# A two-layer hybrid encoder trunk: keys, values and first queries projected before the gate input

## The chip, the cores and the metric

One core of one Trainium2 chip. Times are device microseconds (us) of a whole execution. The kernel before takes 1126.06 us, the median of three runs (1125.95 to 1127.46).

## The reference, cut to what matters

Each of the two layers normalises its input, projects it to 1792 columns and splits them into queries, keys and values for an attention group and two gate inputs for a gating group:

```python
h = rms_norm(x, attn_norm_g[i])
proj = h @ w_in[i]
q, k, v, u, vv = jnp.split(proj, split_at, axis=-1)
q = axial_rope(rms_norm(q.reshape(b, s, N_HEADS, HEAD_DIM), q_norm_g[i]), tables)
k = axial_rope(rms_norm(k.reshape(b, s, N_KV_HEADS, HEAD_DIM), k_norm_g[i]), tables)
attn_o = gqa_attention(q, k, v)
sg_o = spatial_gating(jax.nn.gelu(u), jax.nn.gelu(vv), sg_norm_g[i], sg_w[i], sg_b[i])
merged = concatenate([rms_norm(attn_o, attn_out_g[i]), rms_norm(sg_o, sg_out_g[i])])
x = x + merged @ w_o[i]
# then a second norm, an up-projection, a depthwise convolution, SiLU gate, a down-projection
```

There are 512 positions, width 1024, 8 query heads and 2 key/value heads of 64, and 8 gating heads of 64. `spatial_gating` norms vv per head and mixes it over 128 positions. Attention and gating meet only at `merged`.

## The kernel before, in words

Products keep float32 accuracy by splitting each operand into a rounded high part and a low rest: three matmuls stand for one (`mm3`, lines 259 to 261). Weights come as chunks of at most 128 x 1024 on SP's DMA queue (line 108), in the order of `chunk_plan`. ScalarE makes the high part (line 123); the low part (line 125) is made by VectorE, or by GpSimd in two halves for the chunks of u, of the second queries (a2) and of the output projections. There are 4 raw and 6 split buffers, and splitting runs 3 chunks ahead of use.

A layer projects in four groups: `vv`, the gate input (512 columns); `a1`, the 2 key heads, 4 query heads and the 2 value heads together (512); `u`, the gating multiplier (512); `a2`, the other 4 query heads (256). `in_group` runs the first two as blocks of 4 chunks, 8 weight blocks by 4 position blocks, 96 matmuls, into four PSUM banks. In the first group (flag True) the weight blocks come one after the other over all position blocks, since x is still arriving in layer 0. After it `row_rsqrt` makes the row scale r with a small matmul and a Newton chain on VectorE (lines 213 to 218).

*Gate chain*: gelu on ScalarE (line 419), squares (398), their sums on VectorE (399), a Newton chain of 12 small operations (400, 213 to 218), a multiplication by the norm on VectorE (407), by the gain on GpSimd (409), and the split into high part on ScalarE (410) and rest on VectorE (411). *Key chain*: squares (326), sums (327), 14 small operations (331 to 336), scaling out of PSUM (339), value copies (432, 433), and rotations (349 to 355): the keys and one pair of query heads on VectorE, another pair on GpSimd.

What follows is written out by hand in the string `PROG_AT`, which `run` walks: U is a unit of six u matmuls (16 of them), K transposes the rotated keys and splits them into stacks (`k_stacks`, lines 386 and 387), Q does so for a pair of query heads (375, 376), C is a block of scores with its exponential on ScalarE (470) and scaling on GpSimd (472), T transposes probabilities (489), M mixes the gate input with the spatial weights. K stands behind nine U, the first C behind all sixteen, the first M behind eight C.

Every engine works through its instructions in the order in which the build put them, which follows the order of the code up to small moves. So the order in which the two chains are written sets their order on VectorE, ScalarE and GpSimd. PSUM has 8 banks from one pool; 25 small and 8 large SBUF buffers are shared.

Of the kernel before, what the change touches and what calls it, by code (L numbers as in the profile page):

```python
# [13 lines left out]
AF = mybir.ActivationFunctionType  # L14
# [7 lines left out]
NT = S // P  # L22
# [27 lines left out]
def ffn_order():  # L50
    order = []
    ng = len(GROUPS)
    for g in range(ng):
        lo = sum(GROUPS[:g])
        for j in range(lo, lo + GROUPS[g]):
            order.append(("up", j))
            if g > 0 and j == lo + 1 and g < ng - 1:
                order.append(("dn", g - 1))
    order.append(("dn", ng - 2))
    order.append(("dn", ng - 1))  # L60
    return order


def chunk_plan():
    plan = []
    for l in range(DEPTH):
        for nm in ("vv", "a1", "u", "a2"):
            plan += [((nm, l, i), IN_K[nm] * IN_W[nm]) for i in range(KT // IN_K[nm])]
            if nm == "a2":
                plan.append((("ws", l, 0), NH * P))  # L70
        for nm in ("so", "ao"):
            plan += [((nm, l, c, i), 1024) for c in range(2) for i in range(2)]
        for kind, i in ffn_order():
            if kind == "up":
                plan += [(("up", l, i, h), 1024) for h in range(2)]
            else:
                n, w = GROUPS[i], GCOLS[i]
                plan += [(("dn", l, i, q, h), n * w // 2) for q in range(D // w) for h in range(2)]
    return plan


PLAN = chunk_plan()
CH = 1024

# [67 lines left out]
def trunk_kernel(ctx: ExitStack, tc: tile.TileContext, xT, wts, pk, gq, rope, out):  # L152
    nc = tc.nc
    V, A, G, T = nc.vector, nc.scalar, nc.gpsimd, nc.tensor
# [10 lines left out]
    def k2(name="k2", dt=F32):  # L165
        return k2p.tile([P, 512], dt, tag="k2", name=name)

    def k8(name="k8", dt=F32):
        return k8p.tile([P, 4, 512], dt, tag="k8", name=name)

    def ps(name="ps"):
        return psp.tile([P, 512], F32, tag="ps", name=name)

    def tn(n, name, dt=F32):
        return tiny.tile([P, n], dt, tag=f"tiny_{name}_{n}", name=name)
# [34 lines left out]
    def rsqrt(v, y, n, name):  # L210
        t = tn(n, name + "t", I32)
        a = tn(n, name + "a")
        V.tensor_scalar(out=t, in0=v.bitcast(I32), scalar1=1, scalar2=None, op0=ALU.logical_shift_right)
        V.tensor_scalar(out=y.bitcast(I32), in0=t, scalar1=-1, scalar2=0x5F3759DF, op0=ALU.mult, op1=ALU.add)
        for _ in range(3):
            V.tensor_tensor(out=a, in0=y, in1=y, op=ALU.mult)
            V.scalar_tensor_tensor(out=a, in0=a, scalar=-0.5, in1=v, op0=ALU.mult, op1=ALU.mult)
            V.scalar_tensor_tensor(out=y, in0=a, scalar=1.5, in1=y, op0=ALU.add, op1=ALU.mult)
# [9 lines left out]
    def row_rsqrt(acc, width, name):  # L228
        bank = ps()
        for b in range(NT):  # L230
            T.matmul(bank[:, b:b + 1], lhsT=acc[:, b * P:(b + 1) * P], rhs=ones[:, 0:1], start=(b == 0), stop=(b == NT - 1))
        v = tn(NT, name + "v")
        V.tensor_scalar(out=v, in0=bank[:, 0:NT], scalar1=1.0 / width, scalar2=EPS, op0=ALU.mult, op1=ALU.add)
        r = tn(NT, name + "r")
        rsqrt(v, r, NT, name)
        return r
# [21 lines left out]
    def mm3(out, lh, ll, rh, rl, start, stop):  # L258
        T.matmul(out, lhsT=lh, rhs=rh, start=start, stop=False)  # L259
        T.matmul(out, lhsT=lh, rhs=rl, start=False, stop=False)  # L260
        T.matmul(out, lhsT=ll, rhs=rh, start=False, stop=stop)  # L261
# [4 lines left out]
    for l in range(DEPTH):  # L266
# [32 lines left out]
        def in_group(nm, korder, hooks=None):  # L299
            width = IN_W[nm]  # L300
            banks = [ps(f"{nm}_{b}") for b in range(NT)]
            for c in range(4):
                w = ws.next((nm, l, c))
                wv = w[:, :, 0:2 * width].rearrange("p t (k n) -> p t k n", k=2)
                if korder:
                    seq = [(k, b) for k in range(2) for b in range(NT)]
                else:
                    seq = [(k, b) for b in range(NT) for k in range(2)]
                if korder and c == 0:
                    hi, lo = xs[0]  # L310
                    for lt, rt, first in ((hi, 0, True), (lo, 0, False), (hi, 1, False)):
                        for b in range(NT):
                            T.matmul(banks[b][:, 0:width], lhsT=lt[:, b * P:(b + 1) * P], rhs=wv[:, rt, 0], start=first, stop=False)
                    seq = seq[NT:]
                for k, b in seq:
                    kt = c * 2 + k
                    hi, lo = xs[kt]
                    sl = slice(b * P, (b + 1) * P)
                    mm3(banks[b][:, 0:width], hi[:, sl], lo[:, sl], wv[:, 0, k], wv[:, 1, k], kt == 0, kt == KT - 1)
                if hooks and c in hooks:  # L320
                    hooks[c]()
            return banks
# [21 lines left out]
        def rope_pair(eng, qn, h0, ti):  # L344
            src = qn[:, :, h0 * HD:(h0 + 2) * HD].rearrange("p b (h d) -> p b h d", h=2)
            rot, tmp = k2("rot"), k2("rtmp")
            r4 = rot.rearrange("p (b h d) -> p b h d", b=NT, h=2)
            t4 = tmp.rearrange("p (b h d) -> p b h d", b=NT, h=2)
            eng.tensor_tensor(out=r4, in0=src, in1=tab[:, 2 * ti].unsqueeze(2).to_broadcast([P, NT, 2, HD]), op=ALU.mult)
            for hf in range(2):  # L350
                for sw in range(2):
                    o, s_ = hf * 32 + sw * 16, hf * 32 + (1 - sw) * 16
                    eng.tensor_tensor(out=t4[:, :, :, o:o + 16], in0=src[:, :, :, s_:s_ + 16],
                                      in1=tab[:, 2 * ti + 1, :, o:o + 16].unsqueeze(2).to_broadcast([P, NT, 2, 16]), op=ALU.mult)
            eng.tensor_tensor(out=rot, in0=rot, in1=tmp, op=ALU.add)
            return rot
# [34 lines left out]
        vvx, kk, rots = {}, [], {}  # L391

        def vv_stat():
            vvg = vvx["g"]
            ss = tn(NT * NH, "ssv")
            for b in range(NT):
                sq = k2("sq")
                A.activation(out=sq, in_=vvg[:, b], func=AF.Square)
                V.reduce_sum(out=ss[:, b * NH:(b + 1) * NH], in_=sq.rearrange("p (h d) -> p h d", h=NH), axis=AX.X)
            V.tensor_scalar(out=ss, in0=ss, scalar1=1.0 / HD, scalar2=EPS, op0=ALU.mult, op1=ALU.add)  # L400
            vvx["r"] = tn(NT * NH, "rsv")
            rsqrt(ss, vvx["r"], NT * NH, "sv")
            vvx["h"], vvx["l"] = k8("vh", F32R), k8("vl", F32R)

        def vv_norm(b):
            vvg, rs, vh, vl = vvx["g"], vvx["r"], vvx["h"], vvx["l"]
            V.tensor_tensor(out=vvg[:, b].rearrange("p (h d) -> p h d", h=NH), in0=vvg[:, b].rearrange("p (h d) -> p h d", h=NH),
                            in1=rs[:, b * NH:(b + 1) * NH].unsqueeze(2).to_broadcast([P, NH, HD]), op=ALU.mult)
            G.tensor_tensor(out=vvg[:, b], in0=vvg[:, b], in1=sgn_bc, op=ALU.mult)
            A.activation(out=vh[:, b], in_=vvg[:, b], func=AF.Copy)  # L410
            V.tensor_tensor(out=vl[:, b], in0=vvg[:, b], in1=vh[:, b].bitcast(F32), op=ALU.subtract)

        vb = in_group("vv", True)
        r = row_rsqrt(sqacc, D, "rx")
        r2 = tn(NT, "r2")
        V.tensor_tensor(out=r2, in0=r, in1=r, op=ALU.mult)
        vvx["g"] = k8("vvg")
        for b in range(NT):
            A.activation(out=vvx["g"][:, b], in_=vb[b], func=AF.Gelu_apprx_tanh, scale=r[:, b:b + 1])
        vv_stat()  # L420
        for b in range(NT):
            vv_norm(b)

        ab = in_group("a1", False)
        ssq1 = tn(NT * 6, "qass")
        for b in range(NT):
            qk_stat(ssq1, ab[b], b, 6)
# [7 lines left out]
        krot = rope_pair(V, qn1, 0, 1)  # L435
        rots[0] = rope_pair(G, qn1, 2, 0)
        rots[1] = rope_pair(V, qn1, 4, 0)

        wa2 = []
        ssq2 = tn(NT * 4, "qbss")  # L440
# [372 lines left out]
```

## Time and profile before

| | |
|---|---|
| median of the runs | 1126.06 us |
| span of the profiled execution | 1123.4 us |
| TensorE busy | 1085.4 us (97%) |
| VectorE busy | 801.9 us (71%) |
| ScalarE busy | 502.2 us (45%) |
| GpSimd busy | 224.0 us (20%) |
| HBM traffic over the span | 88 GB/s |

The profile gives the execution's span, from its first to its last instruction; the runs' times hold what lies around it too. The busy shares are means over two layers whose attention parts look unlike their feed-forward parts: of the 40 slices of the span, VectorE is busy over 80% in the second, third and fourth (28 to 112 us) and again at the start of layer 1. The execution is best read around the places where TensorE stops. The trace calls TensorE PE, VectorE DVE, ScalarE ACT, GpSimd POOL.

### The profile page before, as it was taken

The numbers are of one execution on the slowest core, as the hardware profiler recorded it, in microseconds if no ns is written. First come the engines' busy times: TensorE is split into PE (matmuls) and PEld (weight loads), VectorE is DVE, ScalarE is ACT, GpSimd is POOL, SyncE is SP. The second block draws the span as 40 slices with busy tenths as digits, with TensorE's granted clock in tenths as the row PEclk, the third lists the DMA queues.
The fourth block names the chain that finished last, engine by engine and source line by source line (L and its number), as shares of the span: only waits on it lengthen the run. The fifth ranks groups of instructions, "written<-read, shape, count | busy, mean of one in ns | idle before, by whom it ended". The sixth has DMA issues, their size and how long they took to land.

```text
span 1123.4 us, 13306 instructions
## 1 busy us (share of the span) xinstructions
PE 1085.4 (97%) x5024; PEld 903.1 (80%) x5024; DVE 801.9 (71%) x1210; ACT 502.2 (45%) x786; POOL 224.0 (20%) x221
## 2 busy tenths in 40 slices
PE   9969899999999999999999789999999999999998
PEld 7859687788888888888888688787888888888887
DVE  7898998787753777347668899977877447763573
ACT  6348683454431444224344586644444124441330
POOL 6665642200000000000166564421000000000000
PEclk9989999999999999999999899999999999999999
DMA  7321103232323323232332220122232322323201
GB/s 263 121 94 57 38 1 111 77 106 82 113 89 99 96 92 113 76 111 94 97 114 74 76 76 1 38 75 95 94 113 79 109 94 94 107 81 113 88 25 75
DMA packets 29439, 99.76 MB, mean 89 GB/s; under 512 B 3392, under 2 KB 4032, under 8 KB 29376
## 3 DMA queue, kind: packets, MB, share of 16 engines
q1 hardware_dynamic: 29088, 98.79, 26.3%
q8 instruction: 39, 0.64, 0.2%
q14 instruction: 24, 0.20, 0.1%
q10 hardware_dynamic: 288, 0.14, 0.0%
HBM read 96.82 MB, written 2.10 MB: 88 GB/s over the span
## 4 chain that ended last, share of the span: by engine, by line
PE 71%; DVE 7%; ACT 1%; issue 1%; POOL 1%; DVEq 0%; ACTq 0%
PE dn L261 7%; PE dn L260 7%; PE dn L259 7%; PE upg L260 7%; PE upg L261 7%; PE upv L261 7%; PE upv L259 7%; PE upv L260 7%; PE upg L259 7%; PE pT L489 1%; DVE wspl L125 1%; DVE xl L255 1%; PE vv L260 1%; PE vv L259 1%; PE vv L261 1%
## 5 line engine op out<-in xcount | busy, mean ns | idle before, releaser
L123 ACT ACTIVATE wspl<-wraw 128x1024 fp32r<-128x1024 f32 (+1 forms) x207 | 191.8, 938 | 249.9 <-PE dn L261 136.7
L125 DVE TENSOR_TENSOR wspl<-wraw,wspl 128x1024 fp32r<-128x1024 f32 (+1 forms) x151 | 191.4, 1269 | 92.7 <-ACT wspl L123 92.5
L259 PE MATMUL upg<-xh,wspl 128*128 128x512 f32 x352 | 137.4, 390 | 2.1 <-ACT xh L254 2.1
L260 PE MATMUL upg<-xl,wspl 128*128 128x512 f32 x352 | 137.2, 390 | 1.1 <-DVE xl L255 1.1
L261 PE MATMUL upv<-xh,wspl 128*128 128x512 f32 x352 | 137.0, 389 | 0.0
L260 PE MATMUL upv<-xl,wspl 128*128 128x512 f32 x352 | 137.0, 389 | 0.0
L261 PE MATMUL upg<-xh,wspl 128*128 128x512 f32 x352 | 137.0, 389 | 0.0
L259 PE MATMUL upv<-xh,wspl 128*128 128x512 f32 x352 | 136.9, 389 | 0.0
L259 PE MATMUL dn<-g,wspl 128*128 128x512 f32 x352 | 136.9, 389 | 0.0
L260 PE MATMUL dn<-g,wspl 128*128 128x512 f32 x352 | 136.9, 389 | 0.0
L261 PE MATMUL dn<-g,wspl 128*128 128x512 f32 x352 | 136.9, 389 | 0.0
L671 ACT ACTIVATE ht<-ht,pk_sb 128x512 f32<-128x512 f32 x88 | 70.9, 808 | 69.0 <-DVE ht L669 69.0
L708 DVE TENSOR_TENSOR x<-x,dn 128x512 f32<-128x512 f32 x63 | 43.0, 685 | 66.3 <-PE dn L261 66.2
L672 DVE SCALAR_TENSOR_TENSOR ht<-ht,pk_sb 128x511 f32<-128x511 f32 x88 | 65.7, 747 | 33.0 <-ACT ht L671 33.0
L125 POOL TENSOR_TENSOR wspl<-wraw,wspl 128x512 fp32r<-128x512 f32 x56 | 77.6, 1408 | 49.8 <-ACT wspl L123 49.8
L259 PEld LDWEIGHTS upg<-xh,wspl 128*128 128x128 f32 x352 | 66.1, 188 | 16.5 <-ACT xh L254 2.9
L260 PEld LDWEIGHTS upg<-xl,wspl 128*128 128x128 f32 x352 | 66.1, 188 | 15.6 <-DVE xl L255 2.1
L682 ACT ACTIVATE g<-ht 128x512 fp32r<-128x512 f32 x44 | 27.7, 631 | 110.8 <-DVE ht L678 110.8
L261 PEld LDWEIGHTS upv<-xh,wspl 128*128 128x128 f32 x352 | 66.1, 188 | 13.8
L259 PEld LDWEIGHTS upv<-xh,wspl 128*128 128x128 f32 x352 | 66.1, 188 | 13.7
L259 PEld LDWEIGHTS dn<-g,wspl 128*128 128x128 f32 x352 | 66.1, 188 | 13.7
L260 PEld LDWEIGHTS dn<-g,wspl 128*128 128x128 f32 x352 | 66.1, 188 | 13.7
(198 smaller groups left out, 2049.5 us busy)
## 6 DMA issues: line engine op xcount, KB each, us to landing
wraw<-in_wts SPq DMA_DIRECT2D x177, 512.0 KB, 3.4
x<-in_xT SPq DMA_DIRECT2D x8, 256.0 KB, 6.0
out_y<-x SPq DMA_DIRECT2D x7, 256.0 KB, 2.0
wraw<-in_wts SPq DMA_DIRECT2D x2, 256.0 KB, 3.9
sgn<-in_gq SPq DMA_DIRECT2D x2, 256.0 KB, 4.7
rope<-in_rope SPq DMA_DIRECT2D x2, 256.0 KB, 4.9
pk_sb<-in_pk SPq DMA_DIRECT2D x1, 208.0 KB, 7.2
gq_sb<-in_gq SPq DMA_DIRECT2D x2, 64.0 KB, 5.1
```

Source lines behind the costliest of these rows:

```text
L123: nc.scalar.activation(out=t[:, 0, e], in_=raw[:, e], func=AF.Copy)
L125: lo.tensor_tensor(out=t[:, 1, e], in0=raw[:, e], in1=t[:, 0, e].bitcast(F32), op=ALU.subtract)
L255: V.scalar_tensor_tensor(out=lo, in0=x_sb[d], scalar=gcol, in1=hi.bitcast(F32), op0=ALU.mult, op1=ALU.subtract)
L259: T.matmul(out, lhsT=lh, rhs=rh, start=start, stop=False)
L260: T.matmul(out, lhsT=lh, rhs=rl, start=False, stop=False)
L261: T.matmul(out, lhsT=ll, rhs=rh, start=False, stop=stop)
L489: T.transpose(bank[:, b * P:(b + 1) * P], pt[b][:, s * P:(s + 1) * P], ident)
L671: A.activation(out=tt, in_=h, func=AF.Identity, scale=col(PK_CW + 2 * NCT + ct), bias=col(PK_CB + ct))
L672: V.scalar_tensor_tensor(out=tt[:, 1:S], in0=h[:, 0:S - 1], scalar=col(PK_CW + ct), in1=tt[:, 1:S], op0=ALU.mult, op1=ALU.add)
L682: A.activation(out=hi, in_=t[0], func=AF.Copy)
L708: V.tensor_tensor(out=x_sb[dt], in0=x_sb[dt], in1=bank, op=ALU.add)
```

## The change

In each layer the group `a1` is projected first, and its chain is written behind it; then `vv` and the gate chain. The plan of the weight chunks is changed to match. The first group runs with the flag True as before, the second with False. The u units, a2 and the string `PROG_AT` stay as they are. In the changed kernel the lines of the moved code have other numbers: the gate's gelu is line 434 instead of 419, the value copies are 424 and 425 instead of 432 and 433.

```diff
-        for nm in ("vv", "a1", "u", "a2"):
+        for nm in ("a1", "vv", "u", "a2"):
...
-        vb = in_group("vv", True)
+        ab = in_group("a1", True)
         r = row_rsqrt(sqacc, D, "rx")
         r2 = tn(NT, "r2")
         V.tensor_tensor(out=r2, in0=r, in1=r, op=ALU.mult)
-        vvx["g"] = k8("vvg")
-        for b in range(NT):
-            A.activation(out=vvx["g"][:, b], in_=vb[b], func=AF.Gelu_apprx_tanh, scale=r[:, b:b + 1])
-        vv_stat()
-        for b in range(NT):
-            vv_norm(b)
-
-        ab = in_group("a1", False)
         ssq1 = tn(NT * 6, "qass")
...
         rots[1] = rope_pair(V, qn1, 4, 0)
+
+        vb = in_group("vv", False)
+        vvx["g"] = k8("vvg")
+        for b in range(NT):
+            A.activation(out=vvx["g"][:, b], in_=vb[b], func=AF.Gelu_apprx_tanh, scale=r[:, b:b + 1])
+        vv_stat()
+        for b in range(NT):
+            vv_norm(b)
```

VectorE in layer 0, from the second rotation to the key and query stacks. Before (rot and rtmp are the rotated pair and its helper, wspl a weight split, here that of the mixing weights, kk and qs the stacks):

```order
L355 TENSOR_TENSOR rot<-rot,rtmp 128x512
L353 TENSOR_TENSOR rtmp<-qn,tab 128x8x16 x4
L125 TENSOR_TENSOR wspl<-wraw,wspl 128x1024
L355 TENSOR_TENSOR rot<-rot,rtmp 128x512
L387 TENSOR_TENSOR kk<-tr,kk 64x512 x2
L376 TENSOR_TENSOR qs<-tr,qs 64x512
```

After (ssv are the gate's sums of squares, vvg the gate input, vl its low part; nine of the twelve small operations are left out):

```order
L353 TENSOR_TENSOR rtmp<-qn,tab 128x8x16 x4
L355 TENSOR_TENSOR rot<-rot,rtmp 128x512
L399 TENSOR_REDUCE ssv<-sq 128x8 x4
L400 TENSOR_SCALAR ssv<-ssv 128x32
L213 TENSOR_SCALAR svt<-ssv 128x32
...
L218 SCALAR_TENSOR_TENSOR rsv<-sva,rsv 128x32
L407 TENSOR_TENSOR vvg<-vvg,rsv 128x512 x4
L411 TENSOR_TENSOR vl<-vvg,vh 128x512 x4
L125 TENSOR_TENSOR wspl<-wraw,wspl 128x1024
L387 TENSOR_TENSOR kk<-tr,kk 64x512 x2
L376 TENSOR_TENSOR qs<-tr,qs 64x512
```

The gate chain, which stood ahead of the whole key chain, now stands between the last rotation and the stacks.

GpSimd in layer 0, from the first u splits to the scaling of the first probabilities. Before (sgn is the gate's gain, p a block of probabilities):

```order
L125 TENSOR_TENSOR wspl<-wraw,wspl 128x512 x6
L409 TENSOR_TENSOR vvg<-vvg,sgn 128x512 x2
L125 TENSOR_TENSOR wspl<-wraw,wspl 128x512
L409 TENSOR_TENSOR vvg<-vvg,sgn 128x512 x2
L125 TENSOR_TENSOR wspl<-wraw,wspl 128x512 x5
L349 TENSOR_TENSOR rot<-qn,tab 128x512
L353 TENSOR_TENSOR rtmp<-qn,tab 128x8x16 x4
L355 TENSOR_TENSOR rot<-rot,rtmp 128x512
L125 TENSOR_TENSOR wspl<-wraw,wspl 128x512 x6
L472 TENSOR_SCALAR p<-p,sm 128x512 x8
```

After:

```order
L125 TENSOR_TENSOR wspl<-wraw,wspl 128x512 x6
L349 TENSOR_TENSOR rot<-qn,tab 128x512
L353 TENSOR_TENSOR rtmp<-qn,tab 128x8x16 x4
L355 TENSOR_TENSOR rot<-rot,rtmp 128x512
L125 TENSOR_TENSOR wspl<-wraw,wspl 128x512 x6
L409 TENSOR_TENSOR vvg<-vvg,sgn 128x512 x4
L125 TENSOR_TENSOR wspl<-wraw,wspl 128x512 x6
L472 TENSOR_SCALAR p<-p,sm 128x512 x8
```

The rotation moves ahead of six weight splits (the last u chunk and the two of a2), and the gate's four multiplications, now in a row, behind them.

## Rows read from the trace of the kernel before

**Rows 1.** Waits of TensorE: who waited for whom, total us, times, longest.

```profile
PE tr L361 <- DVE rot L355: 17.1, 2, 9.4
```

**Rows 2.** Busy us by engine in a stretch, then granted clock, DMA share, GB/s.

```profile
76.00:78.00 2.00, 2.00 (x6) 1.41 (x6) 2.00 (x3) 0.66 (x2) 1.27 (x1) 0.50 0.00 0
```

**Rows 3.** Timeline of TensorE, layer 0: start, us, line, out<-in, count, [idle before].

```profile
52.58 0.39 PE L259 MATMUL u<-wspl,xh 128*128 128x512 f32 x1
...
74.42 1.08 PE L361 MATMUL tr<-ident,rot 128*128 128x128 f32 x4 [9.44 <-DVE rot L355]
...
87.50 0.39 PE L466 MATMUL sc<-kk,qs 128*128 128x512 f32 x1
...
96.88 1.03 PE L489 MATMUL pT<-ident,p 128*128 128x128 f32 x8
```

**Rows 4.** The same, layer 1.

```profile
628.04 1.09 PE L361 MATMUL tr<-ident,rot 128*128 128x128 f32 x4 [7.71 <-DVE rot L355]
...
640.84 0.39 PE L466 MATMUL sc<-kk,qs 128*128 128x512 f32 x1
```

**Rows 5.** Timeline of VectorE, layer 0.

```profile
37.39 0.17 DVE L416 TENSOR_TENSOR r<-rxr 128x4 f32<-128x4 f32 x1
40.36 2.47 DVE L399 TENSOR_REDUCE ssv<-sq 128x8 f32<-128x512 f32 x4 [2.81 <-ACT sq L398]
42.86 0.95 DVE L400 TENSOR_SCALAR ssv<-ssv 128x32 f32<-128x32 f32 x1
...
47.35 4.69 DVE L407 TENSOR_TENSOR vvg<-vvg,rsv 128x512 f32<-128x512 f32 x4
...
58.75 1.92 DVE L327 TENSOR_REDUCE qass<-sq 128x6 f32<-128x384 f32 x4
...
64.01 0.18 DVE L216 TENSOR_TENSOR qaa<-qaf 128x24 f32<-128x24 f32 x1
...
66.25 1.95 DVE L339 TENSOR_TENSOR qn<-a,qaf 128x384 f32<-128x384 f32 x4
68.12 0.86 DVE L433 SCALAR_TENSOR_TENSOR vs<-a,rxr,vs 128x128 fp32r<-128x128 f32 x3
...
76.09 1.21 DVE L125 TENSOR_TENSOR wspl<-wraw,wspl 128x1024 fp32r<-128x1024 f32 x1
...
78.91 0.67 DVE L387 TENSOR_TENSOR kk<-tr,kk 64x512 fp32r<-64x512 f32 x1
```

**Rows 6.** The same, layer 1.

```profile
590.55 0.16 DVE L416 TENSOR_TENSOR r<-rxr 128x4 f32<-128x4 f32 x1
...
601.55 4.68 DVE L407 TENSOR_TENSOR vvg<-vvg,rsv 128x512 f32<-128x512 f32 x4
...
611.47 0.69 DVE L411 TENSOR_TENSOR vl<-vvg,vh 128x512 fp32r<-128x512 f32 x1 [0.15 <-ACT vh L410]
```

**Rows 7.** Timeline of ScalarE, both layers.

```profile
87.70 0.69 ACT L606 ACTIVATE u<-u,rxr 128x512 f32<-128x512 f32 x1 [0.65 <-PE u L261]
...
90.74 0.69 ACT L470 ACTIVATE p<-sc,m 128x512 f32<-128x512 f32 x1
...
586.63 1.28 ACT L419 ACT_TABLE_LOAD   x1
...
642.78 1.28 ACT L470 ACT_TABLE_LOAD   x1
644.08 0.69 ACT L470 ACTIVATE p<-sc,m 128x512 f32<-128x512 f32 x1
```

**Rows 8.** Timeline of GpSimd, layer 0.

```profile
42.48 2.54 POOL L125 TENSOR_TENSOR wspl<-wraw,wspl 128x512 fp32r<-128x512 f32 x2 [6.33 <-ACT wspl L123]
...
51.45 1.73 POOL L125 TENSOR_TENSOR wspl<-wraw,wspl 128x512 fp32r<-128x512 f32 x1
...
71.94 1.79 POOL L355 TENSOR_TENSOR rot<-rot,rtmp 128x512 f32<-128x512 f32 x1
...
92.13 5.38 POOL L472 TENSOR_SCALAR p<-p,sm 128x512 f32<-128x512 f32 x8 [0.60 <-DVE sm L471]
```

## The prediction

> **What bounds the kernel now.** I read the waits of TensorE first. Its longest wait by far is that for the rotated keys: 17.1 us in two waits, one per layer, the longest 9.4 [rows 1]. The timeline of TensorE places it: in layer 0 the key transposes (step K of the program) start at 74.42 after 9.44 us idle, in layer 1 at 628.04 after 7.71 [rows 3, 4]. So TensorE would have reached K at 64.98 and 620.33. The granted clock is the second half of the price: it reads 0.50, the 1.2 GHz level, while TensorE works again from 76 to 78 us [rows 2]; the engine had been idle before it fell.
>
> The reader then follows what K waits for, on VectorE [rows 5]. The keys are squared, scaled and rotated there from 58.75 on, behind all of the gate input's work, which holds the engine from 40.36 to 58.75. K is late because this queue is served in the order in which the projections are written, and the gate input, which comes first, is needed only by the mixing matmuls after the first scores.
>
> What runs on TensorE behind K: from the first u matmul (52.58) to K without its wait (64.98) lie nine u units, 1.38 us each. Seven more and three transpose groups lie between K and the first scores: 7 x 1.38 and 3 x 0.4 (an estimate: one took 1.08 at the lower clock) = 10.8 us. The first scores could then start at 75.8 instead of 87.50, and in layer 1 at 631.1 instead of 640.84 [rows 3, 4]: **11.7 and 9.7 us**, the clock's part included. That is the most that TensorE's own work allows.
>
> **The change, part by part.** No instruction is added or removed; weight loads have the same sizes and the same order on SP's queue. Both projections are 512 columns wide, so the 0 to 52.58 us of TensorE stay. What moves is the order on VectorE, ScalarE and GpSimd.
>
> *Keys first.* Their chain can start once the row scale r is there, 37.56 us now (37.39 + 0.17) [rows 5]. The four sums of squares of the keys (1.92 us from 58.75) now stand before and inside the small operations that make r, and the split of the third u chunk (two GpSimd instructions, 2.54 us, [rows 8]) falls there too, since ScalarE no longer has the gate's gelu in front of it. Of this I take 2.4 us: r at 40.0. Bounds: 0 and 4.5, the sum of both.
> Then 14 small operations. They took 5.6 us (60.67 to 66.25), the first four of them 3.3, while GpSimd was splitting weights; the last ten, undisturbed at 0.18 each, took 2.24 (64.01 to 66.25). At that pace fourteen take 3.1, and I take that, GpSimd having nothing to do until the keys are scaled (bounds 3.1 and 5.6). Scaling takes 1.87 (66.25 to 68.12). Value copies and the two rotations on VectorE ran from 68.12 to 78.91, less a weight split of 1.21 that now comes later: 9.6. Sum: 40.0 + 3.1 + 1.9 + 9.6 = 54.6. K wants the rotated keys at 64.98: **the wait of 9.44 goes**, with 10 us to spare.
>
> *Gate second.* Here is what is late next. The key and query stacks (the split of the transposed keys, L387) stand behind the whole gate chain in VectorE's queue, as they stood before, but the chain now ends just before them. TensorE ends the gate projection at 52.58; gelu and square of the last bank with a weight split between them end at 54.6. Four sums of squares take 2.5: 57.1. Twelve small operations: 4.5 in the trace (42.86 to 47.35), 2.7 at the undisturbed pace; the last split of the second-query weights on GpSimd falls into them, as one did before, so I take 4.3: 61.4. The gate's norm and split ran from 47.35 to 58.75, 11.4 us, and in layer 1 from 601.55 to 612.16, 10.6, each with a GpSimd weight split of some 1.73 among the four multiplications [rows 5, 6, 8]; in the new order GpSimd does the four in a row, and I take the second less the split, 8.9 (bounds 8.9 and 11.4): 70.3. The mixing weights' split, 1.2: **the stacks start at 71.5**, now 78.91.
>
> From the stacks to the first exponential ScalarE needed 11.83 us (78.91 to 90.74), of which 0.65 was waiting for the last u matmul [rows 7], which is over by then: 11.2, so 82.7, which is 8.0 earlier. The scores themselves find their keys ready 2.6 us into the stacks (74.1, wanted at 75.8), so they don't wait; they then run out of PSUM banks, which the u gelus and exponentials free. What counts behind it is the first transposed probabilities (96.88): the last of the four that they need is the sixth GpSimd scaling, 92.13 + 6 x 0.67 = 96.15 [rows 3, 8], so 0.7 us of slack is used up as well. TensorE arrives there **8.0 + 0.7 = 8.7 us earlier** instead of 11.7: some 3 us come back as new waits before that point.
>
> *Layer 1.* r is there at 590.7 [rows 6]; 17.3 us later (as above, with 5.8 for the small operations, since the third u split falls among them here) VectorE is through with the rotations at 608.0, and the gate projection ends at 607.9 (620.33 - 12.4). The last sum of squares ends 2.7 us after that, since ScalarE has no weight split between; 4.8 for the small operations, 8.9, 1.2: stacks at 625.5. First exponential 11.2 later, 636.7, now 644.08 [rows 7]: 7.4, and the same 0.7 of slack: **8.1 us**.
> The load of the gelu table, 1.28 us at 586.63, lay hidden in ScalarE's wait for r [rows 7]. Now it stands in front of the first gate gelu, by TensorE's pace between 603.8 and 605.1; that bank is ready at 604.1, but the last of the four only at 608.2, and by then ScalarE has caught up: nothing.
> The Trainium skill (ScalarE: Activation LUTs, What ACT_TABLE_LOAD costs) gives 2.66 us for a switch, the load and a drain of about 1.38. By that ScalarE would be 1.4 us late at the last bank and the time 1.4 us longer; the trace shows no such drain behind the load before layer 1's first exponential (642.78 + 1.28 = 644.06, the exponential at 644.08, [rows 7]).
>
> **Sum.** 8.7 + 8.1 = 16.8 us. The profiled execution has a span of 1123.4; the median of the runs is 1126.06, 2.7 more, which I take as what lies around it and as unchanged. 1126.06 - 16.8 = **1109.3 us**, span 1106.6. The sum depends on the stack's start nearly one to one; I trust it to 2 us a layer. Its low ends together (r 2.4 and small operations 1.6 earlier) give 67.5, and then TensorE's own work is the bound. After the stage nothing is moved, so the other waits of TensorE should stay.
>
> **Rivals.**
> *TensorE is the bound (20%).* If the gate chain is 3 us a layer shorter than I have it, all of 11.7 + 9.7 = 21.4 us is won: 1104.7. For it: the undisturbed pace of the small operations. Against it: VectorE and GpSimd both have work nearly all the time from 40 to 80 us.
> *Half of it comes back (13%).* The bounds taken at their upper ends: r 2.1, small operations 2.5, norm 2.5 more, 7.1 in all at worst; with 4 us a layer the gain is 8.8: 1117.3. For it: GpSimd's six splits and the rotation, queued ahead of the gate's multiplications. Against: their inputs are early.
> *Slower (5%).* VectorE operations with two operands in SBUF could be held for every GpSimd instruction that runs beside them. Between r and the stacks GpSimd does ten weight splits of 1.27 and a rotation of 5.6 us (68.12 to 73.73, [rows 5, 8]), 18.3 in all; the sum above holds 4 of it in r and the gate's small operations, and I take 3 more to be inside the rotations' measured 9.6. The other 11.3 would put the stacks at 82.8 and 636.8, the exponentials 3.3 and 3.9 us later than now, TensorE 2.6 and 3.2 later at the transposes: 1131.9. It turns from a gain to a loss when the gate chain is over 8 us longer than summed. Against it: the rotations, which the sum has at their measured price, ran with GpSimd at work beside them and are not stretched that far.
> The Trainium skill (SBUF — State Buffer, the section with the single rule on the shared port pair) says exactly this: the pair is locked for a whole instruction and the other engine blocks. The trace agrees where four small operations took 3.3 us beside a split and ten without one 2.24 [rows 5]; it doesn't show it for whole stretches.
> *No net change (4%).* The wait moves entirely to the first scores, which would need stacks at about their old time; the same chain with 7 us more: within 1 us of 1126.
>
> **How the numbers follow.** The forecast has 58%, with a range of its own of 1105.5 to 1113. The other 42% lie as given. To leave out no more than 2 in 10 the range takes in the bound by TensorE and half of the third case: 1102 to 1118. About 0.2% (2.2 us) is what a measurement can tell here: faster 0.91, same 0.03, slower 0.06.
>
> **What would show it.** In the new profile the wait of TensorE for the rotated keys is gone, and K starts near 65 and 620 us. The granted clock is 1.00 there. The stacks start near 71.5 and 625.5 on VectorE, the first exponential near 82.7 and 636.7, and new short waits of TensorE (1 to 2 us each) stand between the first scores and the first transposed probabilities, on ScalarE or GpSimd. I am wrong if the gate chain on VectorE ends much before or after 70 us, if TensorE waits at the u matmuls for weight splits, or if the mixing matmuls wait for the gate.

## The result and the profile after

In the comparison run the changed kernel takes 1114.46 us in the median (1110.32 to 1124.39) and the kernel before 1127.09 (1125.95 to 1134.05): a ratio (of the means) of 0.9896, 95% interval 0.9864 to 0.9928. By the medians it is faster by 12.6 us, where 16.8 was forecast; 1109.3 lies 5.2 below the median and 1.0 below the fastest execution. The median lies in the stated range of 1102 to 1118, but above the forecast's own of 1105.5 to 1113. The profiled execution is one of the longer ones: 1121.61 us, span 1119.7, mean granted clock 0.986.

The waits of TensorE (total us, times, longest), answering to [rows 1]:

```profile
PE pT L489 <- DVE att L505: 4.9, 2, 2.5
PE ps L231 <- DVE asq L524: 4.1, 2, 2.1
PE sc L466 <- DVE qs L376: 2.8, 4, 1.1
PE pT L489 <- ACT p L470: 2.7, 2, 1.4
...
PE sc L466 <- ACT u L606: 0.9, 2, 0.6
```

The 17.1 us for the rotated keys are gone, and nothing of that size has come in their place. New are the waits of the scores (sc): four for the split queries of 2.8 us together, and two short ones for the u gelus. Two waits for weight splits at the start of layer 0 (13.51 and 19.16, 1.5 us together) are new too, but the two projections end only 0.12 us later than before, at 52.70. The wait for asq, the sums of squares of the attention output, was there before; it matters below. (Two of the expectations call it the gate's; line 524, which it waits for, adds up squares of the attention output.)

The timeline of TensorE in layer 0, answering to [rows 3]:

```profile
64.95 0.60 PE L361 MATMUL tr<-ident,rot 128*128 128x128 f32 x4
...
77.16 0.50 PE L466 MATMUL sc<-kk,qs 128*128 128x512 f32 x1 [1.10 <-DVE qs L376]
...
78.72 0.47 PE L466 MATMUL sc<-kk,qs 128*128 128x512 f32 x1 [0.82 <-DVE qs L376]
...
91.63 1.03 PE L489 MATMUL pT<-ident,p 128*128 128x128 f32 x8
```

The key transposes start at 64.95 without a wait, 9.5 us earlier; the first transposed probabilities, at 91.63, only 5.25 earlier. VectorE in the same stretch, answering to [rows 5]:

```profile
38.63 1.20 DVE L416 TENSOR_TENSOR r<-rxr 128x4 f32<-128x4 f32 x1
...
42.91 1.95 DVE L339 TENSOR_TENSOR qn<-a,qaf 128x384 f32<-128x384 f32 x4
44.78 1.12 DVE L425 SCALAR_TENSOR_TENSOR vs<-a,rxr,vs 128x128 fp32r<-128x128 f32 x4
...
50.95 5.29 DVE L353 TENSOR_TENSOR rtmp<-qn,tab 128x128 f32<-128x128 f32 x4
56.28 1.67 DVE L355 TENSOR_TENSOR rot<-rot,rtmp 128x512 f32<-128x512 f32 x1
57.87 2.45 DVE L399 TENSOR_REDUCE ssv<-sq 128x8 f32<-128x512 f32 x4
60.35 0.18 DVE L400 TENSOR_SCALAR ssv<-ssv 128x32 f32<-128x32 f32 x1
...
63.04 4.69 DVE L407 TENSOR_TENSOR vvg<-vvg,rsv 128x512 f32<-128x512 f32 x4
...
72.25 2.31 DVE L125 TENSOR_TENSOR wspl<-wraw,wspl 128x1024 fp32r<-128x1024 f32 x1
74.48 0.67 DVE L387 TENSOR_TENSOR kk<-tr,kk 64x512 fp32r<-64x512 f32 x1
```

Up to the scaled keys it goes as forecast (r at 39.83; 40.0 was forecast). Then four small multiplications of the second rotation take 5.29 us. GpSimd (answering to [rows 8]) splits weights all that time, and again beside the mixing weights' split:

```profile
50.45 8.65 POOL L125 TENSOR_TENSOR wspl<-wraw,wspl 128x512 fp32r<-128x512 f32 x6
63.81 6.76 POOL L409 TENSOR_TENSOR vvg<-vvg,sgn 128x512 f32<-128x512 f32 x4 [4.71 <-DVE vvg L407]
71.83 3.87 POOL L125 TENSOR_TENSOR wspl<-wraw,wspl 128x512 fp32r<-128x512 f32 x2 [1.26 <-ACT wspl L123]
```

Layer 1 on TensorE, answering to [rows 4]:

```profile
622.50 0.60 PE L361 MATMUL tr<-ident,rot 128*128 128x128 f32 x4
...
633.45 0.39 PE L466 MATMUL sc<-kk,qs 128*128 128x512 f32 x1
```

Again no wait for the keys. But without its wait the kernel before would have come to this point at 620.33, 2.2 us earlier than the changed kernel does, although the latter left layer 0's attention 5.25 us ahead. So 7.4 us were lost on the way, where the change moved nothing. The granted clock shows where. It reads 0.50 behind the wait for asq, as long again behind two waits of the up-projection for the split x (from 212 us), and half as long at a wait for att (from 116 us). At the first scores, ahead of the point where the 5.25 us were taken, it falls as well (us, busy us of PE, PEld, DVE, ACT, POOL with counts, granted clock, DMA share, GB/s):

```profile
80.00:82.00 2.00, 1.69 (x4) 0.50 (x2) 0.97 (x2) 1.95 (x5) 1.58 (x2) 0.50 0.00 0
...
168.00:170.00 2.00, 1.94 (x9) 1.97 (x10) 1.25 (x3) 0.00 (x0) 0.00 (x0) 0.50 0.68 248
170.00:172.00 2.00, 2.00 (x5) 1.56 (x6) 1.66 (x11) 0.00 (x0) 0.00 (x0) 0.50 0.00 0
...
214.00:216.00 2.00, 2.00 (x8) 1.90 (x9) 0.62 (x4) 0.89 (x1) 0.00 (x0) 0.50 0.00 0
```

At 0.50, the 1.2 GHz level, the 2 us from 170 hold 5 matmuls where they hold 10 at 1.00 (a row of the same stretch stands with the run e2_fill_ra). In windows of 2 us over the whole span, each counted as (1 - clock) x 4 us of half clock, this profile has 30.7 us of it, that of before 24.0, of which 17.0 lie in and behind the two key waits, about half of that while TensorE stood idle anyway.

All executions that left a span show the same. Changed kernel, us at mean granted clock, from the shortest to the longest:

```
comparison run: 1110.32 at 1.000, 1111.33 at .998, 1114.13 at .997, 1114.19 at .992,
                1114.46 at .994, 1114.80 at .995, 1121.61 at .986, 1121.70 at .988, 1124.39 at .983
after_again:    1110.0 at 1.000, 1113.0 at .997, 1113.58 at .997, 1123.09 at .986,
                1123.93 at .985, 1123.96 at .985, 1125.01 at .983, 1125.25 at .983
```

### The profile page after: what moved, and what is told of

The parts are those of the page before. It is cut to its first block, busy times and chain, and to the rows that moved or that the text cites. A ratio compares the mean times of both kernels' runs of the same rounds, so it can differ in the third digit from the quotient of the medians.

```text
span 1119.7 us, 13310 instructions
## 1 busy us (share of the span) xinstructions
PE 1092.9 (98%) x5024; PEld 905.7 (81%) x5024; DVE 801.6 (72%) x1210; ACT 503.8 (45%) x786; POOL 225.4 (20%) x221
## 4 chain that ended last, share of the span: by engine, by line
PE 76%; DVE 17%; ACT 3%; issue 2%; DMA 0%; POOL 0%; SPq 0%; DVEq 0%; ACTq 0%
PE dn L261 7%; PE dn L259 7%; PE dn L260 7%; PE upg L260 7%; PE upg L259 7%; PE upg L261 7%; PE upv L260 7%; PE upv L261 7%; PE upv L259 7%; DVE wspl L125 2%; PE pT L489 2%; DVE rtmp L353 1%; PE a L260 1%; DVE xl L255 1%; PE so L259 1%
## 5 line engine op out<-in xcount | busy, mean ns | idle before, releaser
L125 DVE TENSOR_TENSOR wspl<-wraw,wspl 128x1024 fp32r<-128x1024 f32 (+1 forms) x151 | 193.7, 1284 | 92.7 <-ACT wspl L123 92.5
L259 PE MATMUL upg<-xh,wspl 128*128 128x512 f32 x352 | 139.0, 395 | 2.1 <-ACT xh L254 2.1
L261 PE MATMUL upg<-xh,wspl 128*128 128x512 f32 x352 | 138.4, 393 | 0.0
L259 PEld LDWEIGHTS upg<-xh,wspl 128*128 128x128 f32 x352 | 67.1, 191 | 16.8 <-ACT xh L254 2.9
L261 PEld LDWEIGHTS upg<-xh,wspl 128*128 128x128 f32 x352 | 67.0, 190 | 14.0
L260 PEld LDWEIGHTS upv<-xl,wspl 128*128 128x128 f32 x352 | 66.4, 189 | 13.9
```

The lines of the kernel that those rows point to most:

```text
L125: lo.tensor_tensor(out=t[:, 1, e], in0=raw[:, e], in1=t[:, 0, e].bitcast(F32), op=ALU.subtract)
```

## The experiments

The runs after_again, e1, e2 and e4 shared one chip and its runs of the kernel before (1128.41 median, 1126.1 to 1134.12); e3, e5 and e6 another (1127.95, 1125.97 to 1128.84). Ratios are of means.

**after_again.** The changed kernel once more, with no edit.

> The changed kernel once more, for its spread and for the granted clock of each execution. Theory (the stage gains some 12 to 16 us, and what differs between executions are stretches at the lower clock): times between 1110 and 1124, and those with a mean clock near 1.00 are the short ones, near 1110. Rival (the executions differ in the stage itself): no order of the times by the clock.

1123.51 in the median, ratio 0.991 (0.987 to 0.995), with the executions above. But for a few neighbours the order by time is the order by clock, as the theory has it; between 1.000 and 0.983 lie 15 us. Where the median falls among these is chance: 1114.46 once, 1123.51 the next time.

**e2_fill_ra.** Nine dummy matmuls in front of the small matmul that waits for asq, in its own bank, which that matmul starts anew:

```
-    def row_rsqrt(acc, width, name):
+    def row_rsqrt(acc, width, name, fill=None):
         bank = ps()
+        if fill is not None:
+            for _ in range(9):
+                T.matmul(bank, lhsT=ones_r, rhs=fill, start=True, stop=True)
...
-            "r": lambda: sgx.update(ra=row_rsqrt(asq[0], 512, "ra")),
+            "r": lambda: sgx.update(ra=row_rsqrt(asq[0], 512, "ra", xs[0][0])),
```

> Changed kernel with nine dummy matmuls (2.0 us) ahead of the small matmul that waits 2.05 us for the sum of squares of the attention output; their result is overwritten. Theory (the lower clock follows a stretch in which TensorE waits): no granted clock of 0.50 behind this place in either layer, and where the changed kernel has one there (168 to 174 us), some 3 us less. Rival (the clock falls whatever TensorE does there): 0.50 appears there as before, or the dummies cost their 2 us.

1110.11 (1108.73 to 1110.56), ratio 0.9829 (0.9807 to 0.9851), clocks 0.995 to 1.000. The spread of 15 us has become one of 2, at its lower end. The same windows in its profile:

```profile
168.00:170.00 2.00, 2.00 (x12) 1.70 (x12) 1.76 (x9) 0.00 (x0) 0.00 (x0) 1.00 0.57 211
170.00:172.00 2.00, 2.00 (x10) 1.65 (x9) 1.79 (x9) 0.00 (x0) 0.00 (x0) 1.00 0.00 0
```

Ten matmuls instead of five in the second. Half clock over the span: 8.6 us instead of 30.7; the span is 11.4 shorter (1108.3), about half the difference, as work at half the clock would have it. So the spread of the changed kernel is the clock's, and with this wait filled it is gone. The dummies do no useful work; they only keep the engine from standing still. Of the three long stretches at half clock that are gone, only one lay behind this wait. The other two (from 212 and 760 us) lay behind the waits for the split x, which nothing fills; the first of these two waits became shorter, 0.54 us instead of 1.03, in both layers. How much of the 13.4 us between the medians of after_again and this run came in this indirect way is not shown.

**e6_before_fill_ra.** The kernel before with the same edit.

> The kernel before with the same nine dummy matmuls before the small matmul of the gate's row scale. It shows what the change alone is worth once the clock behind that place is the same in both (after with the dummies: 1110.1). Theory: the change's own gain, free of the clock there, is what the profile shows up to the first transposed probabilities in the layer where both had the same clock: 7.3 us in layer 1 plus 2.2 lost to stretches, so about 9 a layer at most and 5 at least: before falls only by what it loses to stretches behind that place (it has them less often: its clock there was 1.00 in layer 0's profile), 0 to 5 us, to 1122 to 1127, and the difference to e2 is 12 to 17. Rival: the change's gain is itself the clock's (fewer stretches): then before gains as much as after did, about 13 us, to 1114 or 1115, and the difference is under 6.

1122.75 (1122.06 to 1123.44), ratio 0.9955 (0.9942 to 0.9967). The rival falls. The theory holds at its edges: before falls by 5.2 us (0 to 5 expected), and with both kernels filled the difference is 1122.75 - 1110.11 = **12.6 us** (13.1 with the half microsecond by which the runs of before differ between the two chips; 11.5 to 14.7 between the executions farthest apart). This is the change's own worth: outside the key waits and the tail behind the last matmul the two profiles hold the same 6.8 us of half clock. They also place it. The first eight transposes of probabilities end at 97.42 in e6 and 91.74 in e2 (layer 0), 650.80 and 638.77 (layer 1):

```profile
96.38 1.04 PE L492 MATMUL pT<-ident,p 128*128 128x128 f32 x8
...
649.76 1.04 PE L492 MATMUL pT<-ident,p 128*128 128x128 f32 x8
```

```profile
90.97 0.77 PE L492 MATMUL pT<-ident,p 128*128 128x128 f32 x5 [0.27 <-POOL p L475]
...
638.01 0.76 PE L492 MATMUL pT<-ident,p 128*128 128x128 f32 x5 [0.26 <-POOL p L475]
```

(The first fence is e6, the second e2.) 5.7 us are won in layer 0, 12.0 with layer 1, so 6.3 there; the spans differ by 12.4.

**e3_a2_vector.** The low splits of the second-query weights from GpSimd to VectorE. Two of the six GpSimd splits beside the second rotation are left.

```
-POOL_LO = ("u", "a2", "so", "ao")
+POOL_LO = ("u", "so", "ao")
```

> The changed kernel with the low splits of the second-query weights on VectorE (one of 128x1024 per chunk) in place of GpSimd (two of 128x512). Of the six GpSimd splits in a row from 50.45 to 59.10 us two stay; two splits of 1.2 to 2.3 us come into VectorE's queue among the gate's sums of squares. Theory: the four multiplications of the second VectorE rotation (5.29 us, 1.32 each) are that long because each has a GpSimd split of 1.44 us beside it; with two splits there the four take 3.0 to 3.6 (the first rotation's four, beside GpSimd's own short multiplications, took 1.96). The stacks then start at 74.5 - 2 + 2.4 or a little more, 74.5 to 76. Rival: they are long by themselves (they read the keys' rotation tables and banks that others hold) and stay at 5.0 to 5.3; the stacks then start at 77 or later. The time itself is within 1% of the changed kernel's either way.

1114.65 (1108.96 to 1123.4), ratio 0.9893 (0.9846 to 0.9941): the same spread as the changed kernel's, and no verdict between the two. VectorE, then GpSimd, in its profile:

```profile
51.39 3.09 DVE L353 TENSOR_TENSOR rtmp<-qn,tab 128x128 f32<-128x128 f32 x4
54.51 0.69 DVE L355 TENSOR_TENSOR rot<-rot,rtmp 128x512 f32<-128x512 f32 x1
55.12 1.22 DVE L125 TENSOR_TENSOR wspl<-wraw,wspl 128x1024 fp32r<-128x1024 f32 x1
...
74.01 0.68 DVE L387 TENSOR_TENSOR kk<-tr,kk 64x512 fp32r<-64x512 f32 x1
```

```profile
50.88 3.05 POOL L125 TENSOR_TENSOR wspl<-wraw,wspl 128x512 fp32r<-128x512 f32 x2
```

The four multiplications take 3.09 us instead of 5.29, and the addition behind them 0.69 instead of 1.67. That is the theory (3.0 to 3.6), and the rival (5.0 and more) falls. The two splits that VectorE takes over cost 1.22 each; the stacks start at 74.01, 0.5 earlier than in the changed kernel and a little under the 74.5 to 76 expected.

**e1_stacks_first.** The gate's sums and norm as a step V of TensorE's program behind the first queries, so that VectorE splits the keys and queries first; K and the queries come earlier among the u units.

```
-U00 U01 U02 U03 U10 U12 U13 U20 U11 K U21 Q0 U22 U23 Q1 U30 U31 U32 U33 G0
+U00 U01 U02 U03 K U10 Q0 U11 U12 Q1 V U13 U20 U21 U22 U23 U30 U31 U32 U33 G0
...
-        vv_stat()
-        for b in range(NT):
-            vv_norm(b)
+        def gate_chain():
+            vv_stat()
+            for b in range(NT):
+                vv_norm(b)
...
+            "V": gate_chain,
```

> Changed kernel with the steps K, Q0, Q1 after four to eight u units and the gate chain after its gelu written behind Q1, so that the stacks no longer stand behind the whole gate chain on VectorE. Theory (the time of the stage is set by VectorE's queue: stacks at 74.5 behind the gate chain, exponential at 85.5): the first exponential comes at 79 to 81, TensorE does not wait at the first scores, 8 to 16 us less than the changed kernel's 5 executions' median in the two layers, 1102 to 1107. Rival (what is left over is the clock alone): the first exponential earlier, but the time within 3 us of the changed kernel.

1111.41 (1107.93 to 1113.68), ratio 0.984 (0.9817 to 0.9863). In its profile the stacks start on VectorE at 67.71 and the scores on TensorE at 75.94, without a wait:

```profile
67.71 0.67 DVE L387 TENSOR_TENSOR kk<-tr,kk 64x512 fp32r<-64x512 f32 x1
```

```profile
75.94 0.39 PE L468 MATMUL sc<-kk,qs 128*128 128x512 f32 x1
```

The first exponential comes at 82.05, 3.5 earlier than in the changed kernel but later than the 79 to 81 expected, and the time misses the 1102 to 1107. It is 12.1 us below the median of after_again on the same chip, but only 3.1 below that of the comparison run, and this profile holds 17.0 us of half clock: by the time alone this run does not decide between theory and rival, e5_both does. TensorE's own work up to the first scores ends where the forecast put it (75.8), and none of its waits is at the scores, so the changed kernel's 77.16 and the short waits behind it are the price of the gate chain in front of the stacks.

**e5_both.** e1's order and e2's dummies together.

> The stacks ahead of the gate's norm and split (as in the run e1_stacks_first) together with the nine dummy matmuls before the small matmul of the gate's row scale (as in e2_fill_ra, one bank that is overwritten). Theory: what the changed kernel still loses has two separate parts, the wait of TensorE at the first scores (4.9 us late at the first transposed probabilities in the profile: 91.63 against a forecast of 88.2, and 86.53 in e1) and the half-clock stretches behind the short waits at 168 and 211 us and their like in layer 1. They add up: e1's 1111.4 falls by what its two stretches per layer cost (it ran at clocks .991 to .995), some 4 to 6 us, to 1105 to 1107, at granted clocks of .997 or more and with executions within 3 us of each other. Rival: the two have one and the same gain (in both the engine simply arrives without a gap before the first scores): then no better than e2, 1110, and e1, 1111.

1103.45 (1102.81 to 1105.34), ratio 0.9786 (0.9773 to 0.98), clocks 0.997 to 1.000: a little below the 1105 to 1107 expected. The rival falls: each edit gains on top of the other, 8.0 us over e1 and 6.7 over e2 (6.2 with the half microsecond between the chips). So the stacks' place alone is worth some 3 us a layer. (The expectation's 4.9 us late is 3.4 by the two numbers beside it, 91.63 and 88.2.) This version beats both kernels.

**e4_before_fill.** The kernel before with thirty dummy matmuls in the wait for the keys that add zero to a u bank: they keep TensorE running there.

```
...
+        def k_step():
+            for _ in range(30):
+                T.matmul(ub[1][0:64], lhsT=zero_r, rhs=xs[0][0], start=False, stop=False)
+            kk.extend(k_stacks(transpose4(krot)))
...
-            "K": lambda: kk.extend(k_stacks(transpose4(krot))),
+            "K": k_step,
```

> Kernel before with 30 dummy matmuls (6.8 us, adding zero to a u bank) in the wait for the keys, so that the wait stays and the clock should not fall. Splits the price of the wait: theory (9.4 and 7.7 us of waiting plus some 2.3 and 2 us of matmuls at the lower clock): clock 1.00 behind K, time 3 to 5 us below the kernel before. Rival (the clock's part is nothing, VectorE decides the first scores anyway): same time as before within 1 us, although the clock is 1.00.

1132.85 (1127.51 to 1136.77), ratio 1.0036 (1.0015 to 1.0057). Both forecasts of the time failed: it is 4.4 us above the kernel before, neither 3 to 5 below nor within 1. In layer 0 the clock is kept through most of the wait but falls at its end, and K still waits the last 2.64 us for VectorE:

```profile
74.52 1.09 PE L363 MATMUL tr<-ident,rot 128*128 128x128 f32 x4 [2.64 <-DVE rot L357]
```

```profile
74.00:76.00 2.00, 1.48 (x6) 1.41 (x7) 2.00 (x3) 0.35 (x1) 2.00 (x2) 0.50 0.00 0
```

There the first scores come at 86.80 instead of 87.50 and the first transposed probabilities at 96.17 instead of 96.88, 0.7 us earlier, with part of the lower clock still behind K. In layer 1 only 0.93 us of the wait are left, and the clock reads 1.00 through it and behind it. The key transposes and the first transposed probabilities, here and (the last row, to be read with [rows 4]) in the kernel before:

```profile
634.97 0.63 PE L363 MATMUL tr<-ident,rot 128*128 128x128 f32 x4 [0.93 <-DVE rot L357]
...
655.32 1.15 PE L491 MATMUL pT<-ident,p 128*128 128x128 f32 x8
```

```profile
650.21 1.04 PE L489 MATMUL pT<-ident,p 128*128 128x128 f32 x8
```

From the one to the other TensorE takes 20.35 us instead of 22.17. So the clock behind K was worth 1.8 us there, near the 2 us that the expectation gives it; this part of the theory holds in the one layer where the clock was kept. The profile has more half clock further on than that of before, 37.6 us against 24.0 over the span, and so a longer time; why more, this run does not tell.

## Why the prediction was right, and where it was off

**The wait and its cause: right.** The key wait is gone, K starts at 64.95 without one (64.98 forecast), and the clock is 1.00 there:

```profile
64.00:66.00 2.00, 2.00 (x12) 1.67 (x11) 2.00 (x3) 0.48 (x1) 2.00 (x2) 1.00 0.00 0
```

Of VectorE's chain r (39.83 against 40.0), the small operations (3.04 against 3.1) and the scaling came as summed. The signs for layer 1 (620, 625.5 and 636.7 us) are given on the time axis of the kernel before; less the 8.7 us that the same forecast wins in layer 0 they are 611.6, 616.8 and 628.0. In the profile K starts at 622.50, the stacks at 629.31, the first exponential at 640.38: 3.4 us less won in layer 0, 7.4 lost to the clock on the way, and the stacks 6.8 us behind K, where 5.2 was forecast.

**The term that was mis-sized: the rotations.** Value copies and two rotations were put at 9.6 us, the price in [rows 5], and took 13.1 (44.78 to 57.87). In the kernel before GpSimd was busy with its own rotation beside the first of the two on VectorE and had two single splits beside the second, only one of them beside its multiplications (73.69 to 75.40 in layer 0); with the keys first it still has its rotation beside the first, but then six splits in a row, and they fall on the second. One row groups all sixteen multiplications of L353 on VectorE in both layers (ns: least, median, most), of before and then of after:

```profile
L353 DVE TENSOR_TENSOR rtmp<-qn,tab x16: 273/406/1358, 70.3 to 629.5; 128x128 f32<-128x128 f32 x16
```

```profile
L353 DVE TENSOR_TENSOR rtmp<-qn,tab x16: 544/962/1384, 46.8 to 610.5; 128x128 f32<-128x128 f32 x16
```

The median rises from 406 to 962 ns, and e3 shows that the splits do it. This is a part of the rival "slower", whose mechanism is real and whose size was not: it wanted 11.3 us more in layer 0, and the stacks came 3.0 late, at 74.48 instead of 71.5. The other terms nearly cancel: the gate sums began when the rotations ended (57.87) and not when their inputs were there (54.6), so 3.3 us late; the twelve small operations took 2.7 instead of 4.3, since the splits were over by 59.10; the norm 9.2 instead of 8.9; and the mixing weights' split 2.2 instead of 1.2, again beside GpSimd splits (71.83 to 75.70). 3.3 - 1.6 + 0.3 + 1.0 = 3.0. The rule of the Trainium skill that the prediction weighed (SBUF — State Buffer, Who interferes with whom) also says that a reduction is not held; the four sums of squares took 2.45 us in the changed kernel, half of it beside the last split, and 2.54 (1.86 + 0.68) without one in e3, which agrees.

**What followed from the stacks: right.** From them to the first exponential 11.06 us (11.2 summed), so 85.54 instead of 82.7. The waits before the first transposed probabilities came, 3.7 us in six waits at the scores in both layers, 1.1 us at most where 1 to 2 each were named; and mostly for VectorE's queries, where ScalarE and GpSimd were named. ScalarE, answering to [rows 7]:

```profile
84.25 1.28 ACT L470 ACT_TABLE_LOAD   x1
85.54 0.69 ACT L470 ACTIVATE p<-sc,m 128x512 f32<-128x512 f32 x1
```

Here too the exponential follows the table load at once, so the drain that the Trainium skill (ScalarE: Activation LUTs, What ACT_TABLE_LOAD costs) adds does not show.

**The sum.** With the wait for asq filled in both kernels the change is worth 5.7 + 6.3 us up to the transposed probabilities, 12.6 in the time, where 8.7 + 8.1 = 16.8 was forecast: 3.0 short in layer 0, the 3.0 of the stacks, and 1.8 in layer 1, where the same four multiplications take 5.28 (from 606.59) and the stacks come 1.6 late behind K. That the medians of the comparison run differ by 12.6 as well is partly chance, since both hold half clock.

**What the sum did not hold: the clock behind old waits.** "After the stage nothing is moved, so the other waits of TensorE should stay" is true of the waits and not of what they cost. The wait of 2.05 us for asq stands in both profiles of layer 0; in that of before the clock reads 1.00 behind it (the row below), in that of after 0.50. In layer 1 it is the other way round: 0.50 in that of before (728 to 730), 1.00 in that of after.

```profile
172.00:174.00 2.00, 1.89 (x12) 1.75 (x13) 1.86 (x7) 0.00 (x0) 0.00 (x0) 1.00 0.70 260
```

Both kernels lose there: filled, before falls by 5.2 us, and the changed kernel by 13.4 against its runs on the same chip (4.4 against the median of the comparison run). So the forecast of one number was also one of a clock, and it is in part luck that the median lies in the range: that of after_again, 1123.51, lies outside, as do three of the nine executions of the comparison run. At a clock of 1.000 the changed kernel takes 1110.0 to 1110.3, which is near 1109.3 because two errors oppose: 4.2 us less won by the change, and no half clock, of which the forecast's base had some. What decides in an execution whether the clock falls behind that wait, and whether it falls more often in the changed kernel, stays open.

## What to carry to other kernels

A reordered queue keeps its durations only where its neighbours stay: for each step moved, look which instructions of the other engine will now run beside it, and price it from rows with those neighbours. Before a median is compared with a forecast, put the executions beside their granted clocks; where they spread with the clock, fill the short waits of both kernels and compare again. And a wait that is removed leaves its queue behind: what stands last in it (here the gate's chain before the key stacks) is the next edit, worth another 6 to 7 us.

## What the runs showed of the hardware

- A wait of 2 us can cost more than itself. Behind the wait for asq TensorE ran at half clock for some 6.8 us in the changed kernel's profile (168 to 175), and as long at two places further on that are 1.00 in e2's. Executions of one program differed by 15 us by this, and with nine dummy matmuls in that wait the difference was 2 us.
- Dummy matmuls in a wait are no sure gain: in the long wait for the keys they kept the clock in one layer, where that gave back 1.8 us, and in the other moved its fall to the wait's end, and the kernel got 0.4% slower.
- VectorE multiplications of 128x128 took 0.27 us at best and up to 1.38 beside GpSimd's 128x512 splits, while the splits took 1.44 each (8.65 for six) instead of 1.27: both engines pay, the short instruction far more.
